# Down-projection of a hybrid decoder layer: the last group's right columns as seven products instead of eight

## The chip, the cores and the metric

The kernel runs on one core of a Trainium2 chip. The metric is device time in microseconds (us) of one execution. Before the change it is 1039.08 us, the median of three runs (1039.08 to 1039.49). The profiled execution took 1039.66 us, of which 1037.9 us lie between its first and its last instruction (the span).

## The reference

One decoder layer, all in float32, 256 positions, width 2048, hidden width 5632:

```python
h = rmsnorm(x, g_mix)
z = h @ w_in                       # gated conv, causal pooling, cross-attention
x = x + concat(conv, pool, att) @ w_out
h = rmsnorm(x, g_ffn)
u = causal_dwconv(h @ w_up, ffn_conv_w) + ffn_conv_b
gate, val = split(u, 2)
x = x + (silu(gate) * val) @ w_down
return rmsnorm(x, g_final)
```

The change touches only the last matrix product, `(silu(gate) * val) @ w_down`: 256 rows by 5632 by 2048.

## The kernel before, in words

**Numbers.** TensorE (PE) multiplies in a reduced float32 form. So every float32 operand is split into two, hi and lo = x - hi, and a product of two operands is three matmuls: hi by hi, hi by lo, lo by hi. One matmul takes a 128x128 stationary block (activations) and streams a 128x512 block (weights). For each weight tile of 128 x 2048 elements (4 x 512), ScalarE (ACT) writes hi and VectorE (DVE) then writes lo; this is "the split" of a tile.

**The stream.** All weight tiles stand in one list, `stream`, in the order in which PE uses them. `next_tile` takes the next one; before it does, it issues the loads up to three tiles ahead and the splits up to two ahead (`LOAD_AHEAD`, `SPLIT_AHEAD`). hi and lo have three buffers each, so the split of tile k can only begin when PE is through with tile k - 3. Tiles of `w_up` are loaded into the tag `raw`, three buffers too.

**Up-projection.** The hidden width is cut into 11 units of 512 (`UNITS` = 2, 2, 2, 2, 2, 1 units in six groups). One unit is eight tiles: four for the gate half (w = 0), then four for the value half (w = 1). One tile is 24 matmuls (`up`, line 981): two blocks of 128 rows, four inner blocks, three matmuls each. After the fourth tile of a half, ACT copies PSUM to z and `up_finish` is put on the list `todo`; it is taken off that list after the next tile's first row block. `up_finish` turns z on PE (eight transposes `pz`, line 1079), runs the three-tap convolution on ACT and DVE (lines 1087 and 1089), and multiplies gate and value.

**Down-projection of five groups.** A group of two units gives an activation block of 256 rows by 1024, and its part of `w_down` is 1024 by 2048. That is taken as two blocks of columns, p = 0 (left 1024) and p = 1 (right 1024). Within one, activations (a11, a12, a21, a22) and weights (b11, b12, b21, b22) are 2x2 blocks, and seven products replace eight. `make_forms` builds the sums of activations once per group, `sums`: index 0 is a11, 1 to 4 are sums, 5 is a12, 6 is a22, and for the last group 7 is a21. One product is 12 matmuls (`prod`, line 921), after which DVE adds the PSUM result to `xt` or subtracts it (line 927).

**The weight sums** are made in place, in three buffers of the tile `ffn` (`rawd`), by `Blocks.split`. In order of the products 0 to 6 the split reads:

| product | reads | what its split issues afterwards |
|---|---|---|
| 0 | b11 | DVE: b11 += b12 (line 247); then POOL's queue: an accumulating DMA b12 += b22 from memory (line 244) |
| 1 | b11 + b12 | DVE: b11 += b22 |
| 2 | b11 + b12 + b22 | |
| 3 | b12 + b22 | SP's queue: load b21 over b12 (line 241); POOL's queue: accumulating DMA b11 += b21 |
| 4 | b22 | SP: load the next block's first part |
| 5 | b21 | SP: load the next block's second part |
| 6 | b11 + b12 + b22 + b21 | SP: load the next block's third part |

The next block's parts are b11, b22, b12 in that order; each goes into the buffer that has just been split, so b12 of a block waits for the split of product 6 of the block before.

**The last block** (group 4, p = 1) is of the class `Plain` before the change: four tiles b11, b21, b12, b22 as they are, each split with no sums (lines 281 and 282) and used by `plain` for both row blocks: 24 matmuls a tile (line 1127), 96 in all, and after every second tile two additions to `xt` (line 1136).

**The order around the change.** The list `sched` mixes the tiles of the last unit (u = 10, eight tiles here called U0 to U7) with the products of group 4. `after[t]` says how many products come behind tile t. Before, `after = [0, 0, 0, 1, 1, 1, 2, 6]`. With P0 to P6 the products of the left block and N0 to N3 the four plain tiles, PE's list is: U0 U1 U2 U3 P0 U4 P1 U5 P2 U6 P3 P4 U7 P5 P6 N0 N1 N2 N3. The forms of group 4 are built while U1 and U2 run, since the `up_finish` that completes them is taken off `todo` in U0. The `up_finish` of the last value half is taken off inside N0; it writes `u_last`, which `down_last` needs.

**The end.** `down_last` does the last unit's down-projection in plain form (four tiles, lines 501 to 507 and 1164 to 1166), the final norm and the output.

Which instruction stands where in the queue of PE, ACT and DVE is decided when the program is built, by a planner that goes by program order among what its own estimates show as ready; each engine then runs its queue strictly in that order. Only the first stage and `down_last` are written in a fixed order.

Of the kernel before, what the change touches and what calls it, by code (L numbers as in the profile page):

```python
# [24 lines left out]
def kernel(  # L25
# [25 lines left out]
    def bank(name):  # L51
        return psum.tile([P, 512], F32, tag="bank", name=name)
# [101 lines left out]
    def next_tile():  # L154
        i = state["use"]
        state["use"] += 1
        advance(i + 1 + LOAD_AHEAD, i + 1 + SPLIT_AHEAD)
        return split.pop(i)
# [46 lines left out]
    group_of = []  # L205
# [109 lines left out]
    blocks = []  # L315
    for gi in range(len(group_of) - 1):
        for p in range(2):

            kind = Plain if gi == len(group_of) - 2 and p == 1 else Blocks
            blocks.append(kind(len(blocks), gi, p))  # L320
            if len(blocks) > 1:
                blocks[-2].next = blocks[-1]
# [33 lines left out]
    for gi, (a, n) in enumerate(group_of):  # L356
        n_t = 8 * n
        if not prods:
            after = [0] * n_t
        elif n == 2:  # L360
            after = [0, 0, 0] + [1] * 12 + [2]
        else:
            after = [0, 0, 0, 1, 1, 1, 2, 6]
        assert sum(after) == len(prods)
        for t in range(n_t):
            if gi == 0:
                if t == 0:
                    for o in UP_ORDER:
                        sched.append(("up", 0, o) if isinstance(o, int) else ("mixed", UpBlocks.U, o[1]))
                continue  # L370
            sched.append(("up", a + t // 8, t % 8))
            for _ in range(after[t]):
                sched.append(prods.pop(0))
        if gi < len(group_of) - 1:
            prods = []
            for b in blocks[2 * gi : 2 * gi + 2]:
                n = len(b.ORDER) if isinstance(b, Plain) else N_PROD
                prods += [("plain" if isinstance(b, Plain) else "prod", b, i) for i in range(n)]
# [170 lines left out]
    for k in range(KC):  # L549
        i, j = divmod(k, 4)  # L550
# [347 lines left out]
            tt(form(at, 1), src, form(at, 0).bitcast(F32), op=ALU.subtract)  # L898
        tt(four(1), t, four(0).bitcast(F32), op=ALU.subtract)

    chains = {}

    def prod(bl, i):
        hi, lo = next_tile()

        chain, first, tb, right, op = (
            ("a", True, 0, 0, ALU.add),
            ("b", True, 1, 1, ALU.add),
            ("a", False, 0, 1, ALU.subtract),
            ("a", False, 1, 1, ALU.subtract),  # L910
            ("b", False, 0, 1, ALU.add),
            ("c", True, 0, 0, ALU.add),
            ("a", False, 1, 0, ALU.add),
        )[i]
        if first:
            chains[chain] = bank(f"pp_{bl.gi}_{bl.p}_{chain}")
        ps = chains[chain]
        for j in range(4):
            ah, al = bl.stationary(i, j)
            for n, (a, b) in enumerate(((ah, hi), (ah, lo), (al, hi))):  # L920
                nc.tensor.matmul(  # L921
                    ps, a, b[:, j, :], start=first and j == 0 and n == 0,
                    stop=j == 3 and n == 2, skip_group_check=True,
                )
        c0 = bl.p * 1024 + right * 512
        o = xt[:, tb, c0 : c0 + 512]
        nc.vector.tensor_tensor(o, o, ps, op=op)
# [13 lines left out]
    for o in out_sched:  # L941
        if o[0] == "prod":
            prod(out_blocks, o[1])
            continue
        n2, k, first, last = o
        if first:
            ps = [[bank(f"po_{n2}_{tb}_{n}") for n in range(2)] for tb in range(TB)]
            at_tile = 0
        mm_b(ps, next_tile(), mixT, (k, k + 1), range(TB), first, last)
        at_tile += 1  # L950
        if n2 == 0 and at_tile <= 3:
            out_blocks.load(("b11", "b22", "b12")[at_tile - 1])
        if n2 == 1 and at_tile in (2, 3):
            transpose_in(xt, h2T, "g_ffn", range((at_tile - 2) * 4, (at_tile - 1) * 4), "x2")
        if last:
            add_in(ps, n2 * 2, range(TB), f"o{n2}", ssq4)
# [5 lines left out]
    rawd = [ffn[:, 1 + i, :].rearrange("p (j c) -> p j c", c=512) for i in range(3)]  # L962

    u_last = h2T[:, : 4 * UNITS[-1], :]
    up_ps, up_gates, todo, r_2 = {}, {}, [], []

    def up(u, b):

# [266 lines left out]
    for what, a, b in sched:  # L1235
        {"up": up, "mixed": up_mixed, "prod": prod, "plain": plain}[what](a, b)
# [32 lines left out]
```

## Time and profile before

| what | value |
|---|---|
| median of three runs | 1039.08 us |
| profiled execution | 1039.66 us, span 1037.9 us |
| PE busy | 1026.7 us, 99% of the span |
| DVE busy | 820.5 us, 79% |
| ACT busy | 601.8 us, 58% |
| POOL busy | 64.1 us, 6% |
| DMA moved | 224.97 MB, 217 GB/s on average |
| granted TensorE clock | 0.997 of full speed |

A row of a view of groups gives the source line, the engine, the operation, what it writes and reads, how often, the busy time and the mean of one. A row of a timeline gives start and duration in us, and in square brackets how long the engine had been idle before, and what ended that. PE is the matmuls, PEld its weight loads, SPq the queue of DMA issues. A matmul's own duration (390 ns) is longer than the distance between two, since they overlap; the distance is read from the chain of waits, where 12 of 512 columns take 2.72 us.

### The profile page before, as it was taken

To read this page: it belongs to the slowest core of one execution; us is meant where nothing else is said; L and a number is where in the kernel's file an instruction comes from. 1 tells how busy PE (TensorE), PEld (TensorE's weight loads), DVE (VectorE), ACT (ScalarE), POOL (GpSimd) and SP (SyncE) were. 2 spreads that over 40 slices of the span, in tenths; PEclk is the share of its full clock that TensorE was granted. 3 is DMA by queue.
4 is the path that set the end of the run, shared out by engine and by line. 5 is a ranking of instruction groups with operands and counts; after the bars stand their busy time and mean duration, and the time that the engine had idled before them with its cause. 6 is when DMAs were issued, how large, how long until landed. Compare 5 with 4: busy or idle time off the path is not lost.

```text
span 1037.9 us, 12624 instructions
## 1 busy us (share of the span) xinstructions
PE 1026.7 (99%) x4970; PEld 861.9 (83%) x4970; DVE 820.5 (79%) x866; ACT 601.8 (58%) x654; POOL 64.1 (6%) x97
## 2 busy tenths in 40 slices
PE   9999999999999999999999999999999999999996
PEld 7888888888888888888888888888888888888885
DVE  5677686777869688978779787797878978789776
ACT  5965454544556576655556556665566655665653
POOL 0023500000001000000000000000000000000000
PEclk9999999999999999999999999999999999999998
DMA  9765465557775687687966878668786697867832
GB/s 321 254 214 191 146 201 175 191 191 240 220 262 176 155 259 243 197 253 203 259 224 201 255 204 260 219 199 258 208 260 216 194 265 209 258 218 191 282 118 81
DMA packets 125157, 224.97 MB, mean 217 GB/s; under 512 B 3970, under 2 KB 36010, under 8 KB 124970
## 3 DMA queue, kind: packets, MB, share of 16 engines
q1 hardware_dynamic: 113450, 201.09, 57.2%
q0 software_dynamic: 11616, 23.07, 13.6%
q8 instruction: 39, 0.64, 0.2%
q14 instruction: 20, 0.16, 0.1%
q10 hardware_dynamic: 32, 0.01, 0.0%
HBM read 222.06 MB, written 2.10 MB: 216 GB/s over the span
## 4 chain that ended last, share of the span: by engine, by line
PE 98%; DMA 1%; DVE 0%; SPq 0%; DVEq 0%; issue 0%; ACT 0%
PE pu L981 42%; PE pp_a L921 9%; PE pp_b L921 5%; PE pp_c L921 2%; PE pa_cb L468 2%; PE pa_pv L468 2%; PE pa_cx L468 2%; PE pa_cc L468 2%; PE po L504 2%; PE pp L1127 2%; PE po L501 2%; PE po L507 2%; PE pz L1079 2%; PE pm_a L1024 2%; PE pa_q L468 1%; PE pk L558 1%
## 5 line engine op out<-in xcount | busy, mean ns | idle before, releaser
L981 PE MATMUL pu<-hi,h2T 128*128 128x512 f32 x1280 | 409.4, 391 | 0.0
L132 DVE TENSOR_TENSOR lo<-raw,hi 128x2048 fp32r<-128x2048 f32 (+3 forms) x148 | 314.7, 2128 | 70.9 <-ACT hi L131 69.9
L131 ACT ACTIVATE hi<-raw 128x2048 fp32r<-128x2048 f32 (+3 forms) x148 | 264.3, 1789 | 110.5 <-issue 34.7
L981 PEld LDWEIGHTS pu<-hi,h2T 128*128 128x128 f32 x1280 | 240.3, 188 | 49.4
L981 PE MATMUL pu<-lo,h2T 128*128 128x512 f32 x640 | 249.5, 390 | 0.0
L255 DVE TENSOR_TENSOR lo<-ffn,hi 128x2048 fp32r<-128x2048 f32 x70 | 160.3, 2290 | 72.0 <-ACT hi L254 72.0
L254 ACT ACTIVATE hi<-ffn 128x2048 fp32r<-128x2048 f32 x70 | 134.0, 1916 | 105.1 <-PE pu L981 75.0
L981 PEld LDWEIGHTS pu<-lo,h2T 128*128 128x128 f32 x640 | 120.2, 188 | 25.1 <-DVE lo L132 0.7
L921 PE MATMUL pp_a<-hi,sums 128*128 128x512 f32 x288 | 94.5, 389 | 0.0
L1089 DVE SCALAR_TENSOR_TENSOR t<-pz,cols,t 128x255 f32<-128x255 f32 (+1 forms) x176 | 79.6, 478 | 10.2 <-ACT t L1087 9.2
L1087 ACT ACTIVATE t<-pz,cols 128x256 f32<-128x256 f32 x88 | 46.9, 558 | 48.1 <-DVE t L1089 24.2
L921 PEld LDWEIGHTS pp_a<-hi,sums 128*128 128x128 f32 x288 | 54.1, 188 | 11.2
L244 POOL DMA_DIRECT2D ffn<-in_w_down_dram x18 | 23.1, 1284 | 575.8 <-DVE ffn L247 454.3
L921 PE MATMUL pp_a<-lo,sums 128*128 128x512 f32 x144 | 56.0, 389 | 0.0
L1005 ACT ACTIVATE z<-pu,r_x 128x512 f32<-128x512 f32 x40 | 27.4, 686 | 39.7 <-PE pu L981 39.6
L247 DVE TENSOR_TENSOR ffn<-ffn 128x2048 f32<-128x2048 f32 x20 | 45.7, 2287 | 3.4 <-DMA ffn<-in_w_up_dram 3.4
L921 PE MATMUL pp_b<-hi,sums 128*128 128x512 f32 x144 | 47.3, 389 | 0.0
L921 PEld LDWEIGHTS pp_a<-lo,sums 128*128 128x128 f32 x144 | 27.0, 188 | 5.6
L921 PEld LDWEIGHTS pp_b<-hi,sums 128*128 128x128 f32 x144 | 27.0, 188 | 5.6
L468 PE MATMUL pa_cb<-hT,hi 128*128 128x512 f32 x96 | 30.7, 400 | 0.0
L468 PE MATMUL pa_pv<-hT,hi 128*128 128x512 f32 x96 | 30.2, 396 | 0.0
L468 PE MATMUL pa_cc<-hT,hi 128*128 128x512 f32 x96 | 30.2, 395 | 0.0
(292 smaller groups left out, 1477.1 us busy)
## 6 DMA issues: line engine op xcount, KB each, us to landing
raw<-in_w_up_dram SPq DMA_DIRECT2D x84, 1024.0 KB, 7.5
ffn<-in_w_down_dram SPq DMA_DIRECT2D x40, 1024.0 KB, 6.1
raw<-in_w_in_dram SPq DMA_DIRECT2D x28, 1024.0 KB, 5.0
ffn<-in_w_down_dram POOLq DMA_DIRECT2D x18, 1024.0 KB, 10.3
raw<-in_w_out_dram SPq DMA_DIRECT2D x12, 1024.0 KB, 5.1
raw<-in_w_kv_dram SPq DMA_DIRECT2D x4, 1024.0 KB, 7.3
outp<-in_w_out_dram SPq DMA_DIRECT2D x4, 1024.0 KB, 7.5
ffn<-in_w_up_dram SPq DMA_DIRECT2D x4, 1024.0 KB, 5.5
```

The costliest lines, as they stand in the source:

```text
L131: nc.scalar.activation(hi[:, s, :], raw[:, s, :], AF.Copy)
L132: nc.vector.tensor_tensor(lo[:, s, :], raw[:, s, :], hi[:, s, :].bitcast(F32), op=ALU.subtract)
L244: nc.gpsimd.dma_start(self.buf(to), self.source(what), accum_op=ALU.add)
L247: nc.vector.tensor_tensor(self.buf(to), self.buf(to), self.buf(what), op=ALU.add)
L254: nc.scalar.activation(hi, raw, AF.Copy)
L255: nc.vector.tensor_tensor(lo, raw, hi.bitcast(F32), op=ALU.subtract)
L468: nc.tensor.matmul(ps[mi], hi[:, kk, c], actT[:, k, :], start=first and kk == 0, stop=False)
L921: nc.tensor.matmul(ps, a, b[:, j, :], start=first and j == 0 and n == 0, stop=j == 3 and n == 2, skip_group_check=True,)
L981: nc.tensor.matmul(ps[tb], x_, y_[:, kk, :], start=k == 0 and n == 0, stop=k == KC - 1 and n == 2,)
L1005: nc.scalar.activation(z[tb], ps[tb], AF.Copy, scale=r_2[0][:, tb : tb + 1])
L1087: nc.scalar.activation(t, v, AF.Identity, bias=cvec("ffn_conv_b", m), scale=cw[2])
L1089: nc.vector.scalar_tensor_tensor(t[:, s:], v[:, : S - s], cw[2 - s], t[:, s:], op0=ALU.mult, op1=ALU.add)
```

## The change

The class of the last block becomes `Blocks` like that of the nine before it, so its weights are summed and split by the table above and its seven products (here Q0 to Q6) go through `prod`. The list `after` of the last unit is spread anew for 14 products instead of 7 products and 4 plain tiles. PE's list becomes: U0 U1 U2 P0 U3 P1 U4 P2 P3 U5 P4 P5 U6 P6 Q0 U7 Q1 Q2 Q3 Q4 Q5 Q6, and then `down_last`. The pending `up_finish` is taken off `todo` in Q2, behind its matmuls. The class `Plain`, the function `plain` and the form of index 7 stay in the file; nothing uses the first two, and the form is still made.

```diff
@@ -315,8 +315,7 @@
     for gi in range(len(group_of) - 1):
         for p in range(2):
-
-            kind = Plain if gi == len(group_of) - 2 and p == 1 else Blocks
+            kind = Blocks
             blocks.append(kind(len(blocks), gi, p))
@@ -360,7 +359,7 @@
         elif n == 2:
             after = [0, 0, 0] + [1] * 12 + [2]
         else:
-            after = [0, 0, 0, 1, 1, 1, 2, 6]
+            after = [0, 0, 1, 1, 2, 2, 2, 6]
         assert sum(after) == len(prods)
@@ -898,7 +897,7 @@
-    chains = {}
+    chains, todo = {}, []
@@ -922,6 +921,8 @@
                     stop=j == 3 and n == 2, skip_group_check=True,
                 )
+        if todo and bl.gi == len(group_of) - 2 and bl.p == 1 and i == 2:
+            todo.pop(0)()
         c0 = bl.p * 1024 + right * 512
@@ -962,7 +963,7 @@
-    up_ps, up_gates, todo, r_2 = {}, {}, [], []
+    up_ps, up_gates, r_2 = {}, {}, []
```

## The prediction
> **What bounds the kernel now.** I read the page first, then the chain of waits around the change, then the stretch before and within the last unit by engine.
>
> ```profile
> span 1037.9 us, 12624 instructions
> PE 1026.7 (99%) x4970; PEld 861.9 (83%) x4970; DVE 820.5 (79%) x866; ACT 601.8 (58%) x654; POOL 64.1 (6%) x97
> ```
>
> ```profile
> 942.72 2.72 PE pp_a L921 x12
> 945.44 0.23 PE pu L981
> ...
> 951.81 2.72 PE pp_b L921 x12
> 954.53 5.44 PE pu L981 x24
> ...
> 981.73 2.72 PE pp_a L921 x12
> 984.45 2.72 PE pp L1127 x12
> 987.17 0.88 PE pz L1079 x8
> 988.05 19.05 PE pp L1127 x84
> 1007.11 0.45 PE pl L501 x2
> ```
>
> PE has no gap: each piece starts where the last one ended. So one product of 12 matmuls is 2.72 us, a tile of 24 is 5.44 us, and any wait put on PE lengthens the kernel by itself. P0 starts at 942.72, so U3, 24 matmuls, began at 937.28 and U2 ended there. U4 with its eight transposes runs from 945.44 to 951.81: 6.37 us. The last down-projection starts at 1007.11; what follows it is not touched, so the sum is made on this one point.
>
> ```profile
> 920.00:937.30 17.30, 17.30 (x82) 14.40 (x81) 17.06 (x26) 9.92 (x12) 0.00 (x0) 1.00 0.56 183
> 937.30:1007.10 69.80, 69.80 (x317) 57.89 (x317) 59.83 (x54) 40.97 (x37) 2.56 (x2) 1.00 0.66 196
> ```
>
> By stretches (length, then busy time of PE, PEld, DVE, ACT, POOL, then granted clock, DMA share and GB/s), DVE is not at its mean of 79% here. While U1 and U2 run it is busy 17.06 of 17.30 us, and in the last unit 59.83 of 69.80 us. Its work there, not its average, decides what can be added.
>
> **Removed.** Four plain tiles are 96 matmuls, seven products are 84. Twelve matmuls at 2.72 us per twelve: **-2.72 us** of PE. With nothing else, the down-projection would start at 1004.4. Splits, additions to `xt` and loads of the plain tiles go too, but are replaced.
>
> **Added.** The durations:
>
> ```profile
> L254 ACT ACTIVATE hi<-ffn x70: 1897/1917/1925, 333.3 to 974.3; 128x2048 fp32r<-128x2048 f32 x70
> L255 DVE TENSOR_TENSOR lo<-ffn,hi x70: 2282/2292/2294, 335.6 to 977.2; 128x2048 fp32r<-128x2048 f32 x70
> L247 DVE TENSOR_TENSOR ffn<-ffn x20: 2284/2286/2292, 341.2 to 948.6; 128x2048 f32<-128x2048 f32 x20
> L927 DVE TENSOR_TENSOR xt<-xt,pp_a 128x512 f32<-128x512 f32 x4 | 2.7, 681 | 0.0
> L241 SPq DMA_DIRECT2D ffn<-in_w_down_dram x40: 367/368/368, 377.3 to 983.9; - x40
> DMA to landing us min/median/max: 5.1/6.1/7.7
> L244 POOL DMA_DIRECT2D ffn<-in_w_down_dram x18: 1282/1282/1303, 425.2 to 956.4; - x18
> DMA to landing us min/median/max: 9.2/10.3/11.9
> ```
>
> Seven splits instead of four, two weight additions (line 247) and seven additions to `xt` instead of four. On DVE that is 3 x 2.29 + 2 x 2.29 + 3 x 0.68 = 13.5 us; in the second stretch DVE had 69.80 - 59.83 = 10.0 us idle. So DVE alone can eat the gain: with 2.7 us less room, 16.2 us would have to go into 10.0 us and what can be done after the down-projection has begun. ACT gets 3 x 1.92 = 5.8 us more and had 28.8 us idle there; that is hidden. Two accumulating DMAs (b22 and b21 a second time, 1 MB each) come to POOL's queue, which stood empty after 956.4 us; at 196 GB/s and a DMA share of 0.66 in that stretch there is room for 2 MB.
>
> **The wait at U3.** P0 and P1 come one tile earlier. This is what DVE and ACT did there:
>
> ```profile
> 928.89 2.29 DVE L132 TENSOR_TENSOR lo<-raw,hi 128x2048 fp32r<-128x2048 f32 x1
> ...
> 936.43 0.69 DVE L895 TENSOR_TENSOR turn<-turn,ffn 128x512 f32<-128x512 f32 x1
> 937.03 2.29 DVE L255 TENSOR_TENSOR lo<-ffn,hi 128x2048 fp32r<-128x2048 f32 x1
> 939.23 2.29 DVE L899 TENSOR_TENSOR sums<-turn,sums 128x2048 fp32r<-128x2048 f32 x1
> 941.43 2.29 DVE L247 TENSOR_TENSOR ffn<-ffn 128x2048 f32<-128x2048 f32 x1
> 943.63 2.29 DVE L132 TENSOR_TENSOR lo<-raw,hi 128x2048 fp32r<-128x2048 f32 x1
> 945.84 2.29 DVE L255 TENSOR_TENSOR lo<-ffn,hi 128x2048 fp32r<-128x2048 f32 x1
> ```
>
> ```profile
> 937.15 1.92 ACT L896 ACTIVATE sums<-turn 128x2048 fp32r<-128x2048 f32 x1 [2.26 <-DVE turn L895]
> 943.82 1.92 ACT L254 ACTIVATE hi<-ffn 128x2048 fp32r<-128x2048 f32 x1 [0.37 <-DVE ffn L247]
> ```
>
> In order: lo of U3, the forms up to line 895, lo of P0, the rest of the forms (line 899), the weight addition behind P0, lo of U4, lo of P1. After the change the tile split at 928.89 is P0, and U3's lo comes into the place of 937.03. PE then wants U3 at 940.0 (2.72 us after 937.28) and P1 at 945.4. P1 needs lines 899 and 247 and its own hi and lo. If DVE keeps the order of the rows (U3's lo, 899, 247), 247 ends at 943.7 as now, hi follows to 945.6, lo to 947.9: **P1 waits 2.4 us**. If 247 and 899 go ahead of U3's lo, that ends at 943.6 and U3 waits 3.6 us. If nothing stood between, P1's lo could end at 945.8: 0.4 us. I take 2.4, the order of the rows; the ends 0.4 and 3.6 stay for the range. From here all of PE is 2.4 us later.
>
> **The chain through the weight buffers.** This is the term that decides. In the plain block each tile lasts 5.44 us on PE and needs one load; now Q1 to Q6 stand together at 2.72 us each and hang on each other through memory. Followed from P6:
>
> P6's split waits for a free buffer, the end of P4. P4 would end at 968.1 without a wait (937.28, plus four products and U3, U5 at 2.72 and 5.44, U4 at 6.37, and P4), so at 970.5. hi and lo, 1.92 + 2.29: 974.8. Only then is b12 loaded, 6.1 us: 980.9. DVE adds it to b11, 2.29: 983.2. Then the accumulating DMA b12 += b22, issued 0.3 us later, as this row stands against the end of line 247 at 943.72, and 10.3 us long: 993.8.
>
> ```profile
> 944.02 1.28 POOL L244 DMA_DIRECT2D ffn<-in_w_down_dram  x1 [56.56 <-DVE ffn L247]
> ```
>
> Q3's split, 4.2 us: 998.0. Only then is b21 loaded over it, 6.1 us: 1004.1. Q5's split, 4.2 us: 1008.4. Q5 and Q6, 5.44 us: the down-projection starts at **1013.8**. PE on its own would reach Q5 at 1003.4 (U7 waits for its lo to 985.4, Q1 ends 993.5, Q2's lo ends at 994.0 after b11 += b22, Q3 begins at 998.0, Q4 ends 1003.4), and so stands still for about 5 us before Q5. The sum: -2.72 for the matmuls, +2.4 before P1, +2.2 in small waits from U7 to Q3, +5.0 before Q5, which is 6.9; by the chain 1013.8 - 1007.1 = **+6.7 us**, which I take.
>
> Cover that I count as nothing: the second accumulating DMA (b11 += b21) starts behind Q2's lo at 994.3 and lands at 1004.6, while Q6's hi can start at 1006; if Q5 were on time, this one would hold Q6. For the left block the same steps end in time: b11 += b22 behind P1's lo ends at 950.1, P2's split at 954.3 (when b12 += b22, issued at 944.0, has landed too), P3's at 958.5 against 959.7 on PE; b21 lands at 964.6, before P5's buffer is free. On SP's queue the late load of b21 stands in front of what is issued later, the last tile of the down-projection and the final gains; those need `raw` buffers freed by later splits anyway. On POOL's queue nothing stands behind. On DVE, b11 += b12 waits for b12's landing with the lo of U7 behind it (or ahead of it: then the chain is 2.1 us later, an end for the range; I take the addition first, as in program order). The last `up_finish` starts behind Q2:
>
> ```profile
> 999.74 0.42 DVE L602 TENSOR_TENSOR h2T<-t,h2T 128x256 fp32r<-128x256 f32 x1
> ```
>
> Before, from the transposes at 987.17 to this row, its last, 13.0 us; behind Q2 at 996.6 it ends at 1009.6, four us ahead of the down-projection. Without the wait at Q5 it would be next in line: 992.6 + 13.0 = 1005.6 against 1004.4, so 1.2 us of the 2.7 would go there.
>
> **Ends of the unknown costs.** The two loads 5.1 to 7.7 each, the accumulating DMA 9.2 to 11.9, the early wait 0.4 to 3.6, the order on DVE 0 to 2.1. All at the low end: 6.7 - 1.0 - 1.0 - 1.1 - 2.0 = +1.6 us. All at the high end: 6.7 + 1.6 + 1.6 + 1.6 + 1.2 + 2.1 = +14.8 us. Neither is likely as a whole; about half of either side leaves +3.5 to +10.5.
>
> **Rivals.** A change of under 0.2% (2.1 us) counts as no change, about what a measurement of this kernel can tell.
>
> *The gate on the clock adds to it.* These are stretches after PE's last matmul:
>
> ```profile
> 1028.91 0.28 PE L1166 MATMUL pl<-hi,h2T 128*128 128x256 f32 x1
> ...
> 1031.00:1032.00 1.00, 0.00 (x0) 0.00 (x0) 0.93 (x4) 0.00 (x0) 0.00 (x0) 0.77 0.68 262
> 1032.00:1033.00 1.00, 0.00 (x0) 0.00 (x0) 1.00 (x2) 0.00 (x0) 0.00 (x0) 0.50 0.20 72
> ```
>
> About 2.3 us after PE stopped, its granted clock fell from 1.00 to 0.50. A wait of 5 us before Q5 is longer than that, so Q5 and Q6 could run at half speed: between 0 and 5.44 us more, since no row shows how soon the clock returns. I take the middle, 2.7: +9.4, **1048.5 us**. Against it: if the wait is split into two shorter ones, nothing falls. The Trainium skill, "TensorE: Matmul & The Clock Gate", section "Part 1: The HAM clock gate", says the clock halves after an idle window of about 3.4 us and comes back after as long a busy one. The fall after 2.3 us here is within such a free-running window; by the rule Q5 would lose up to 1.7 us (an estimate from that page), which makes 1047.5.
>
> *All of it is hidden, faster.* Then only the matmuls count: -2.72, or -1.5 with the wait for `up_finish`: 1036.4 to **1037.6 us**. For it: PE has no wait in the whole last unit now, though there ACT did wait for a plain tile's load:
>
> ```profile
> 982.96 1.92 ACT L281 ACTIVATE hi<-ffn 128x2048 fp32r<-128x2048 f32 x1 [1.42 <-DMA ffn<-in_w_down_dram]
> ```
>
>  It decides only if the chain from P6's lo to Q5, 33.6 us, is covered; by the walk PE wants Q5 28.6 us after it (974.8 to 1003.4), and 26.6 us after it with no wait on the way (972.3 to 998.9). It would take both loads and the accumulating DMA at their shortest, the early wait gone, and more.
>
> *Same.* All terms at the low end, +1.6: **1040.7 us**.
>
> *The block doesn't run as seven products in this order.* The planner could move a down-projection tile ahead of Q5; its hi and lo need the buffer of Q4, so little is won, and the last stage has its order written out. I give this nothing of its own.
>
> **How the numbers follow.** The profiled execution took 1039.66 us, 1.76 more than its span, and the median is 0.58 below it. +6.7 gives a span of 1044.6, a profiled execution of 1046.4 and a median of **1045.8 us**. Chances: this chain without the clock 0.52 (its own range 1042.5 to 1049.5), with the clock 0.30 (to 1051.5), worse than that 0.04, same 0.07, faster 0.07. So slower by over 0.2%: 0.86. The range that leaves out less than 2 in 10 runs from the low end of the chain to the chain with the clock: 1040.6 to 1051.5 us.
>
> **What would show it.** In the changed kernel: matmuls of the last block 84, PE busy lower by about 2.7 us while the span is longer; in the chain of waits a step from the accumulating DMA to Q3's hi and one from the load of b21 to Q5's hi, with PE idle 4 to 6 us before Q5; a wait of DVE or ACT for lo or line 247 of 1 to 4 us around 940 to 948; `up_finish` off the chain; perhaps a clock below 1.00 after the wait. It is wrong if PE stays without gaps from U3 to the down-projection, if b12 or b21 of the last block lands before PE wants it, or if the longest wait is for DVE's backlog and not for memory.

## The result, and the profile after

The changed kernel takes **1057.85 us** (median of four runs, 1056.15 to 1058.28) against 1039.09 us for the kernel before on the same chip: a ratio of 1.0176, with a 95% interval of 1.0163 to 1.0188. It is slower by 18.8 us. The forecast was 1045.8 us with a range up to 1051.5: the direction was right, the size was not.

The profiled execution took 1058.03 us, its span is 18.4 us longer than before. The first rows of the profile's page, and its shares of the chain that ended last:

```profile
span 1056.3 us, 12617 instructions
PE 1032.5 (98%) x4958; PEld 864.0 (82%) x4958; DVE 832.8 (79%) x874; ACT 606.7 (57%) x657; POOL 66.7 (6%) x99
PE 87%; DVE 5%; DMA 4%; ACT 2%; issue 1%; SPq 0%; DVEq 0%; ACTq 0%; POOLq 0%
```

The twelve matmuls are gone (4970 to 4958), yet PE is busy for 5.8 us *more*: some matmuls ran at a lower clock. The DMA share of the chain, 4%, lies almost entirely in the last 80 us. This is the chain of waits of the changed kernel there (start, length, what):

```profile
943.48 6.88 PE pu L982 x22
...
975.59 2.21 DVE lo L255
977.80 0.02 issue
977.82 6.22 DMA ffn<-in_w_down_dram
...
986.73 11.42 DMA ffn<-in_w_down_dram
...
1000.17 2.30 DVE lo L255
1002.48 0.02 issue
1002.49 10.41 DMA ffn<-in_w_down_dram
...
1014.95 2.29 DVE lo L255
```

Read from top to bottom: U3's matmuls; P6's lo; the load of b12, landed at 984.04; the accumulating DMA b12 += b22, behind an addition on DVE, landed at 998.15; Q3's lo; the load of b21, landed at 1012.90; Q5's lo. The skeleton is the one that the prediction walked. The last down-projection began at 1007.11 us before. Now its first two matmuls slip in among the first of Q6, but the first that reads a lo part stands at 1025.43 us, behind Q6; before, that one stood at 1007.56, so it is 17.9 us later, nearly the whole difference. PE's own gaps, from its timeline of the changed kernel:

```profile
940.62 0.73 PE L982 MATMUL pu<-hi,h2T 128*128 128x512 f32 x2 [0.92 <-ACT hi L131]
942.42 0.50 PE L920 MATMUL pp_b<-hi,sums 128*128 128x512 f32 x1 [1.07 <-ACT hi L254]
943.48 0.53 PE L982 MATMUL pu<-lo,h2T 128*128 128x512 f32 x1 [0.56 <-DVE lo L132]
...
988.51 0.50 PE L920 MATMUL pp_b<-hi,sums 128*128 128x512 f32 x1 [1.03 <-ACT hi L254]
999.52 0.50 PE L920 MATMUL pp_a<-lo,sums 128*128 128x512 f32 x1 [1.74 <-DVE lo L255]
1004.72 0.50 PE L920 MATMUL pp_b<-lo,sums 128*128 128x512 f32 x1 [2.15 <-DVE lo L255]
...
1014.97 0.50 PE L920 MATMUL pp_c<-hi,sums 128*128 128x512 f32 x1 [3.16 <-ACT hi L254]
1017.29 0.80 PE L920 MATMUL pp_c<-lo,sums 128*128 128x512 f32 x1 [1.82 <-DVE lo L255]
```

Two groups: 2.6 us before U3, and some 10 us from Q1 on. Those gaps are 12.5 us; with the 2.7 us of matmuls saved there are some 8 us more to find. Most of them are matmuls that ran slower, as the stretches show (length, busy time of PE, PEld, DVE, ACT, POOL, granted clock, DMA share, GB/s):

```profile
944.00:948.00 4.00, 4.00 (x13) 3.13 (x12) 4.00 (x3) 0.29 (x2) 0.00 (x0) 0.60 1.09 238
...
1000.00:1016.00 16.00, 10.16 (x36) 7.30 (x34) 10.07 (x14) 6.72 (x11) 1.19 (x1) 0.88 0.59 133
1016.00:1020.00 4.00, 2.71 (x6) 2.15 (x7) 4.00 (x8) 3.88 (x3) 0.00 (x0) 0.50 0.00 0
1020.00:1024.00 4.00, 4.00 (x14) 3.20 (x13) 4.00 (x4) 1.56 (x1) 0.00 (x0) 0.71 0.00 0
```

The granted clock is 0.60 behind the wait at U3 and 0.50 to 0.71 while Q5 runs. Both had to be tested, since a low clock beside a wait may or may not cost anything.

### The profile page after: what moved, and what is told of

Its sections match the earlier page's. It is cut to its first block, busy times and chain, and to the rows that moved or that the text cites. A ratio compares the mean times of both kernels' runs of the same rounds, so it can differ in the third digit from the quotient of the medians.

```text
span 1056.3 us, 12617 instructions
## 1 busy us (share of the span) xinstructions
PE 1032.5 (98%) x4958; PEld 864.0 (82%) x4958; DVE 832.8 (79%) x874; ACT 606.7 (57%) x657; POOL 66.7 (6%) x99
## 4 chain that ended last, share of the span: by engine, by line
PE 87%; DVE 5%; DMA 4%; ACT 2%; issue 1%; SPq 0%; DVEq 0%; ACTq 0%; POOLq 0%
PE pu L982 38%; PE pp_a L920 8%; PE pp_b L920 4%; DMA ffn<-in_w_down_dram 3%; PE pa_cb L467 2%; PE pa_cc L467 2%; PE pa_pv L467 2%; PE pa_cx L467 2%; PE po L506 2%; PE po L500 2%; PE po L503 2%; PE pp_c L920 2%; PE pz L1080 2%; PE pm_a L1025 2%; PE pa_q L467 1%
## 5 line engine op out<-in xcount | busy, mean ns | idle before, releaser
L255 DVE TENSOR_TENSOR lo<-ffn,hi 128x2048 fp32r<-128x2048 f32 x77 | 176.1, 2289 | 78.4 <-ACT hi L254 78.4
L254 ACT ACTIVATE hi<-ffn 128x2048 fp32r<-128x2048 f32 x77 | 147.4, 1915 | 109.2 <-PE pu L982 69.0
L920 PE MATMUL pp_a<-hi,sums 128*128 128x512 f32 x320 | 105.8, 392 | 0.0
L920 PEld LDWEIGHTS pp_a<-hi,sums 128*128 128x128 f32 x320 | 60.7, 190 | 13.1 <-DVE xt L928 0.2
L920 PE MATMUL pp_a<-lo,sums 128*128 128x512 f32 x160 | 62.8, 393 | 1.7 <-DVE lo L255 1.7
L247 DVE TENSOR_TENSOR ffn<-ffn 128x2048 f32<-128x2048 f32 x22 | 50.3, 2285 | 7.3 <-DMA ffn<-in_w_up_dram 3.7
L920 PE MATMUL pp_b<-hi,sums 128*128 128x512 f32 x160 | 53.4, 394 | 2.1 <-ACT hi L254 2.1
L920 PEld LDWEIGHTS pp_a<-lo,sums 128*128 128x128 f32 x160 | 30.3, 189 | 8.2 <-DVE lo L255 2.0
L920 PE MATMUL pp_b<-lo,sums 128*128 128x512 f32 x80 | 31.5, 394 | 2.1 <-DVE lo L255 2.1
L920 PE MATMUL pp_c<-hi,sums 128*128 128x512 f32 x80 | 27.9, 411 | 3.2 <-ACT hi L254 3.2
## 6 DMA issues: line engine op xcount, KB each, us to landing
ffn<-in_w_down_dram POOLq DMA_DIRECT2D x20, 1024.0 KB, 10.4
```

The lines of the kernel that those rows point to most:

```text
L247: nc.vector.tensor_tensor(self.buf(to), self.buf(to), self.buf(what), op=ALU.add)
L254: nc.scalar.activation(hi, raw, AF.Copy)
L255: nc.vector.tensor_tensor(lo, raw, hi.bitcast(F32), op=ALU.subtract)
L920: nc.tensor.matmul(ps, a, b[:, j, :], start=first and j == 0 and n == 0, stop=j == 3 and n == 2, skip_group_check=True,)
```

## The experiments

Four suspects came out of this comparison: the early wait at U3, the chain through memory, the clock, and DVE's queue at the end. The experiments take them apart one by one. Line numbers move by a few where an edit adds lines.

### The early wait alone

The kernel before, with its four plain tiles, and only the list changed: P0 to P3 come one tile earlier, so that P0 and P1 stand where the change has them.

```diff
-            after = [0, 0, 0, 1, 1, 1, 2, 6]
+            after = [0, 0, 1, 1, 1, 1, 1, 6]
```

> The kernel before with its four plain tiles, and only the list of places changed: products start one tile earlier (0, 0, 1, 1, 1, 1, 1, 6), the end of the list as before. Theory (VectorE's backlog in front of U3, about 3.7 us of waiting, and a lower granted clock for the tile after it, about 1.9 us; TensorE has no slack later that could swallow it): 1044 to 1045.5 us. Rival (the early wait is made up later, and only the chain through memory costs): within 1 us of 1039.1.

Measured: 1044.01 us (1043.93 to 1044.18), ratio 1.0044 (1.0027 to 1.0060): **+4.9 us** from the order of the list alone (4.7 against the runs of the kernel before that were taken beside it), twice the 2.4 us of the prediction. In the timeline of DVE of the changed kernel one sees why:

```profile
936.73 2.29 DVE L247 TENSOR_TENSOR ffn<-ffn 128x2048 f32<-128x2048 f32 x1
938.93 2.29 DVE L898 TENSOR_TENSOR sums<-turn,sums 128x2048 fp32r<-128x2048 f32 x1
941.14 2.29 DVE L132 TENSOR_TENSOR lo<-raw,hi 128x2048 fp32r<-128x2048 f32 x1
```

The weight addition and the rest of the forms both went *ahead of* U3's lo. That is the bad end (3.6 us) of the prediction; it took the other order because the rows of before had it. The planner did not keep that order once the tiles were moved.

The opposite edit, the changed kernel with its list begun later:

```diff
-            after = [0, 0, 1, 1, 2, 2, 2, 6]
+            after = [0, 0, 0, 1, 2, 2, 3, 6]
```

> The changed kernel with the list (0, 0, 0, 1, 2, 2, 3, 6): P0 comes behind U3 as in the kernel before, Q0 to Q6 stand where the change put them. Theory (early wait and chain through memory add up, since the chain starts from P6): about 5.5 us less than the change, 1051 to 1054 us. Rival (the chain is tied to something that does not move with TensorE's early wait, such as the accumulating DMAs): 1056 to 1058 us.

Measured: 1054.62 us (1054.37 to 1054.93), ratio 1.0146 (1.0130 to 1.0161): 3.2 us less than the change, not 4.9. The early gaps shrink to two of 0.56 and 0.48 us further on. Yet the chain through memory begins only 1.7 us sooner (P6's lo ends at 976.07 us, not at 977.80), and the accumulating DMA b12 += b22 happened to take 9.02 us in this profile, not 11.42; so not even the whole 3.2 us can be put down to the list. Of the 18.8 us at most 4.9 are this wait.

### The clock

e1 has the early wait and nothing else, so the clock can be tested there: sixteen matmuls whose result nobody reads stand in the gap before U3 and keep PE running.

```diff
+        if u == n_units - 1 and b == 3:
+            fill = bank("fill")
+            for _ in range(16):
+                nc.tensor.matmul(
+                    fill, h2T[:, 0, :P], h2T[:, 1, :], start=True, stop=True
+                )
```

> The kernel of the first experiment (four plain tiles, products one tile earlier), with 16 matmuls of 512 columns that nobody reads put between P0 and U3, 16 x 0.227 = 3.6 us, into a bank of their own; the wait before U3's second matmul was about that long. The output is unchanged. Theory (the tile behind the wait ran at a lower granted clock because TensorE had stood nearly still; 22 matmuls of U3 took 6.5 instead of 5.0 us): with the wait filled the clock stays at 1.00, U3 takes 5.0 us, and the time falls by 1.2 to 1.8 us to about 1042.5 us. Rival (U3 is slow for another reason, its operands for instance, and the record of the clock only goes with it): the same 1044.0 us or up to 0.5 us more.

Measured: 1042.97 us (1042.76 to 1044.47), ratio 1.0038 (1.0026 to 1.0051): 1.0 us less than e1. The runs of the two overlap, so the saving rests on the chains of waits as well. First that of e1, then that of the kernel with the fill:

```profile
943.59 6.47 PE pu L981 x22
```

```profile
940.00 3.63 PE fill L978 x16
...
944.31 4.99 PE pu L987 x22
```

The same 22 matmuls take 6.47 us behind a gap and 4.99 us behind the fill, where the granted clock is 1.00 in every stretch; the fill itself made U3 begin 0.7 us later. So of the 4.9 us, one to one and a half are the clock, the rest is the wait for DVE. The Trainium skill, "TensorE: Matmul & The Clock Gate", section "Part 1: The HAM clock gate", lists the halved clock as the state after an idle window of about 3.4 us. Here it fell although PE's single gaps were 0.9, 1.1 and 0.6 us with one or two matmuls between them, so a sparse stretch can be enough, and the window, read as one gap, would have missed it.

It does not fall every time. Ten of the profiles have these three gaps, the last of them 0.26 to 0.56 us long (the change, e1, e3, e4, e11 and e13 to e17). In eight the clock fell to about 0.50 behind them, and 22 matmuls took 6.47 to 7.84 us where the chain of waits shows them together. In e14 and e16 it stayed at 1.00 with the same gaps, and they took 5.30 us. The code is the same in this stretch, so one execution can differ from the next by one and a half us or more here, and small differences of medians below have to be read with that in mind.

The same idea in the tail of the changed kernel, 36 unread matmuls in the waits before Q2, Q4 and Q5:

```diff
+            if bl.seq == 9 and i == 5 and j == 0:
+                for _ in range(36):
+                    nc.tensor.matmul(
+                        ps, sums[:, 0, 0, 0, :], h2T[:, 5, :], start=True, stop=True,
...
+                    )
```

> The changed kernel with 36 matmuls that nobody reads, written into Q5's bank before its first product; by the program 9 of them stand in the wait before Q2's second matmul, 7 before Q4's and 20 before Q5. The output is unchanged. Theory (the clock that fell in the waits of the last products costs about 2 us at Q4 and Q3 and about 2 us at Q5, but Q6 waits for its lo until 1021.8 us anyway): the granted clock stays near 1.00 there and the time falls by 1 to 3 us. Rival (the waits end when memory and VectorE deliver, whatever the clock): within 0.7 us of the change, or slower by the matmuls put in.

Measured: 1057.84 us (1055.35 to 1058.75), ratio 1.0172 (1.0156 to 1.0188). The clock rose to 1.00 throughout the tail, and **the time did not move**. The stretches of this kernel, beside those of the changed one above:

```profile
1016.00:1020.00 4.00, 3.05 (x12) 2.17 (x12) 4.00 (x8) 3.70 (x4) 0.00 (x0) 1.00 0.00 0
1020.00:1024.00 4.00, 2.76 (x12) 2.31 (x13) 4.00 (x4) 1.47 (x1) 0.00 (x0) 1.00 0.00 0
```

From 1020 to 1024 PE is busy for 2.76 us where it had been busy for 4.00: it runs faster and then waits. What it waits for is the subject of the last group of runs.

### The chain through memory

First, one accumulating DMA out: b11 += b21 is not read from memory a second time but added on DVE, after Q5's split, from the b21 that has been loaded for Q5.

```diff
-                self.add_far("b11", "b21")
+                if self.seq != 9:
+                    self.add_far("b11", "b21")
+            elif idx == 5 and self.seq == 9:
+                self.add("b11", "b21")
```

> The changed kernel, but in the last block the second accumulating DMA (b11 += b21 from memory) is left out and VectorE adds b21 from its buffer, behind Q5's split. Theory (the load of b21 took 10.4 us instead of 6 because it ran beside that accumulating DMA): the load lands in 5.5 to 6.5 us, and the time falls by 3 to 4 us, to about 1054 us. Rival (a load at this place takes about 10 us by itself): the load still takes 9 to 10.5 us, and the time stays or rises by up to 2.5 us for the addition.

Measured: 1058.59 us (1056.21 to 1059.97), ratio 1.0181 (1.0166 to 1.0196): no gain. That is the rival's time, but not for the rival's reason, since the load did get shorter. Its rows hold the largest single finding. The chain of waits, DVE and PE of this kernel:

```profile
1003.76 6.11 DMA ffn<-in_w_down_dram
```

```profile
1015.91 2.29 DVE L247 TENSOR_TENSOR ffn<-ffn 128x2048 f32<-128x2048 f32 x1
```

```profile
1020.28 0.51 PE L923 MATMUL pp_a<-hi,sums 128*128 128x512 f32 x1 [3.21 <-ACT hi L254]
```

The same load of b21 takes **6.11 us alone and 10.41 us beside the accumulating DMA** that the change issues at 999.91. The 4.3 us won there are lost again, because the addition on DVE stands behind what `up_finish` has in the queue, starts only at 1015.91, and Q6 waits 3.21 us for it. Behind that wait the granted clock is 0.55 to 0.59, and eleven matmuls of Q6 take 4.56 us instead of 2.5. No run puts a plain load in the place of the accumulating DMA, so whether any second transfer would cost as much stays open.

That price stood in the trace of before as well. Here are its DMA issues between 944 and 954 us (KB each, median us to landing), the stretch in which the accumulating DMA of 944.02 runs:

```profile
ffn<-in_w_down_dram POOLq DMA_DIRECT2D x1, 1024.0 KB, 10.5
raw<-in_w_up_dram SPq DMA_DIRECT2D x1, 1024.0 KB, 9.9
raw<-in_w_down_dram SPq DMA_DIRECT2D x1, 1024.0 KB, 5.2
```

A plain load of the same 1024 KB, issued 1.9 us after the accumulating DMA: 9.9 us; one issued 1.4 us before that DMA ended: 5.2. The prediction had used the median of all loads of line 241, 6.1 us.

Next, both plain loads off the chain: b12 of the last block goes early into a buffer that is free by then (`u_raw`), b21 into the buffer that P6 frees; both accumulating DMAs stay.

```diff
             if idx == 0:
                 self.add("b11", "b12")
                 self.add_far("b12", "b22")
+                if last:
+                    self.next.load("b12")
...
-                names = Plain.ORDER if isinstance(self.next, Plain) else ("b11", "b22", "b12")
+                names = ("b11", "b22", "b21" if last else "b12")
                 self.next.load(names[idx - 4])
...
+    class Last(Blocks):
+
+        def buf(self, name):
+            if name == "b12":
+                return u_raw.rearrange("p c t -> p (c t)").rearrange("p (j c) -> p j c", c=512)
+            return rawd[self.at(name)]
...
+            elif idx == 3:
+                self.add_far("b11", "b21")
```

In `Last`, the class of the last block, nothing loads b21 behind Q3's split any more.

> The changed kernel, but the last block's b12 has a buffer of its own (the activations' buffer, free once the forms are built) and is loaded while the left block runs; b21 goes into the buffer that P6 frees, right behind P6's split. Both accumulating DMAs stay. Theory (the chain of loads through one buffer is what holds Q3 and Q5): the load of b12 (6.2 us) and that of b21 (10.4 us) leave the chain; what is left is one accumulating DMA in front of Q3; 1043 to 1046 us with the early wait still in it. Rival (VectorE's backlog or the accumulating DMAs set the end): above 1050 us.

> The experiment with a buffer of its own for b12, and the list (0, 0, 0, 1, 2, 2, 3, 6), so P0 again behind U3. Theory (early wait and what is left of the chain add up): the 4.5 to 5.5 us of the early wait go, 1050.3 to about 1045 to 1046 us. Rival (the second accumulating DMA and VectorE's queue hold the end wherever the block begins): 1048 to 1051 us.

Measured: 1050.26 us (1049.47 to 1052.43), ratio 1.0107 (1.0092 to 1.0122), with the list as changed; 1049.52 us (1048.44 to 1050.07), ratio 1.0097 (1.0083 to 1.0111), with the later list. So the two serial loads are worth **7.6 us**, but the theory had expected 1043 to 1046: something else stands at 1050. And the late list, which had won 3.2 us, now wins no more than 0.7: the costs do not add up, and there is a second floor below the memory.

The bound for all of memory: no accumulating DMA and no load of b21 in the last block; DVE adds b22 in both places and the split of Q3 and Q5 reads b22.

```diff
+            last = self.seq == 9
+            names = ("b11", "b11", "b11", "b12", "b22", "b21", "b11")
+            if last:
+                names = ("b11", "b11", "b11", "b22", "b22", "b22", "b11")
...
+            if last:
+                if idx < 2:
+                    self.add("b11", "b22")
```

> The changed kernel, but the last block does without memory in its sums: both accumulating DMAs and the load of b21 are left out, VectorE's two additions stay but add b22, which lies there in time, and Q3 and Q5 read b22 (so the right half of the output is not the reference's). Splits, additions to xt, products and list are those of the change. Theory (of the 18.8 us, 4.7 are the early wait and the rest is the chain through memory, less 2.7 for the matmuls): the chain goes, 1041 to 1045 us. Rival (dense splits, three buffers of hi and lo and VectorE's queue hold the last six products anyway): 1048 us or more.

> The same without memory in the last block's sums (output of the right half not the reference's), with the list (0, 0, 0, 1, 2, 2, 3, 6). Theory: both costs of the change are gone, what is left is the 2.7 us of matmuls against small waits: 1037 to 1040 us. Rival (as before): 1043 us or more.

Measured: 1049.02 us (1048.56 to 1049.14), ratio 1.0089 (1.0072 to 1.0106), and with the later list 1049.27 us (1047.53 to 1052.51), ratio 1.0097 (1.0074 to 1.0119). The rival held in both. **All of memory is worth 8.8 us** (1057.85 less 1049.02), 7.6 of them in the two plain loads. What stays in e11 is 10 us above the kernel before, with no transfer in the chain of waits from U3 to the down-projection (b12 is still loaded, but nobody reads it). With the later list (e12) that chain still goes through two loads, b21 of the left block (8.56 us) and b22 of the last one (6.14), so the bound is e11.

An attempt to keep the sums right and yet off the DMA queues: b12 early as in e4, and both accumulations as additions on POOL from what is already on the chip, with two lists.

```diff
+        def add_pool(self, to, what):
+            nc.gpsimd.tensor_tensor(self.buf(to), self.buf(to), self.buf(what), op=ALU.add)
...
-                self.add_far("b12", "b22")
+                self.add_pool("b12", "b22")
...
-            elif idx == 3:
-                self.add_far("b11", "b21")
+            elif idx == 2:
+                self.add_pool("b11", "b21")
```

The lines are set against e4 with the later list. The form of index 7, which nothing reads, is not built either.

> As the kernel with b12 in its own buffer and the later start, but in the last block both accumulating DMAs are left out: b12 += b22 and b11 += b21 are added on POOL from the buffers, and the form of index 7, which nobody reads, is not built. Theory (what is left is the accumulating DMAs, 10 to 11 us each from issue, against about 4 to 6 us for the addition on POOL by eight times the 0.6 us that 128x256 took there): 1038 to 1042 us. Rival (VectorE's own work, 13.5 us more in a stretch with 10 us idle, is the bound): 1043 us or more.

> As the kernel with the sums on POOL, with the list (0, 0, 0, 1, 1, 3, 4, 5): five products instead of six behind U7, three between U5 and U6, four between U6 and U7. Theory (with memory off the chain the order matters little as long as each split has time): within 1.5 us of the kernel with the sums on POOL. Rival (the dense products in front of U7 wait for b21 and for VectorE as Q1 to Q6 did): 2 to 5 us slower than it.

Measured: 1057.21 us (1056.53 to 1058.29), ratio 1.0176 (1.0160 to 1.0192), and 1058.36 us (1055.93 to 1059.25), ratio 1.0180 (1.0166 to 1.0194). As slow as the change. POOL and DVE of the first of them:

```profile
981.63 6.59 POOL L250 TENSOR_TENSOR ffn<-ffn 128x2048 f32<-128x2048 f32 x1 [25.57 <-DVE ffn L247]
```

```profile
981.46 2.29 DVE L132 TENSOR_TENSOR lo<-raw,hi 128x2048 fp32r<-128x2048 f32 x1
...
984.25 6.11 DVE L258 TENSOR_TENSOR lo<-ffn,hi 128x2048 fp32r<-128x2048 f32 x1
```

POOL's addition lasts 6.59 us, and beside it a lo that takes DVE 2.29 us takes 6.11. The rows show the two taking turns: POOL's began 0.17 us after a lo on DVE, which ended at 983.75; from there to POOL's end at 988.22 it is 4.47 us, and DVE's next lo, begun at 984.25, ends 2.14 us behind that. In e10, where no such row ran on DVE when POOL began, the addition takes 4.54 us, within the 4 to 6 that had been expected. So the engines do not work side by side here: the two additions of e8 hold DVE up by 3.8 us and by 4.4 us (three lo in 11.06 us from 995.20 on), and what leaves memory comes back as time of DVE. The Trainium skill, "SBUF — State Buffer", section "Who interferes with whom", says that a DVE instruction with two inputs from SBUF contends with a GpSimd (POOL) instruction that reads SBUF; these rows agree.

### What stays without memory

In e11 the last product comes late, though its data are on the chip. DVE of that kernel, then PE:

```profile
1002.09 2.28 DVE L259 TENSOR_TENSOR lo<-ffn,hi 128x2048 fp32r<-128x2048 f32 x1
1004.29 1.64 DVE L1097 SCALAR_TENSOR_TENSOR t<-pz,cols,t 128x255 f32<-128x255 f32 x4
...
1010.23 2.29 DVE L259 TENSOR_TENSOR lo<-ffn,hi 128x2048 fp32r<-128x2048 f32 x1
```

```profile
1010.25 0.73 PE L507 MATMUL pl<-hi,h2T 128*128 128x512 f32 x2 [1.39 <-ACT hi L131]
1012.57 0.61 PE L927 MATMUL pp_a<-lo,sums 128*128 128x512 f32 x1 [1.36 <-DVE lo L259]
```

From the end of Q5's lo (1002.09 and 2.28 us on) to the start of Q6's (1010.23) 5.9 us pass on DVE, nearly all with rows of the last `up_finish` and one pause of 0.57 us inside it. PE waits 1.39 and 1.36 us in two gaps before Q6's lo and then runs Q6 at a granted clock of 0.60. The test: the eight taps (line 1097 there) of the last value half are left out.

```diff
-            for s in (1, 2):
+            for s in (1, 2) if (u, w) != (10, 1) else ():
```

> The kernel without the last block's memory chain (label e11_no_memory_chain, 1049.02 us), with the eight tap instructions of the last value half left out on DVE as well, so the last half's convolution has one tap of three and the output is not the reference's. There DVE's rows run without a gap from 1004.29 to 1010.23 through six taps, four multiplications and three lo parts of up_finish, and the last product's lo comes only then (1010.23 to 1012.52), though its hi had been ready since 1007.02. Theory: the 8 us that stay without memory come mostly from DVE's queue, in which the last up_finish stands between the splits. Eight taps of about 0.40 us each are 3.2 us; the last product then starts 3 us sooner, and without the slower clock behind the wait perhaps 4: 1045 to 1046 us. Rival: the buffers of hi and lo and the planner's order set the end (the last product's hi waits for the matmuls of Q3, 1.87 us), so DVE is only where the wait shows: 1048 us or more.

Measured: 1045.00 us (1043.93 to 1046.31), ratio 1.0057 (1.0042 to 1.0072): **4.0 us** less than e11, for eight instructions of 0.4 to 0.5 us. From Q2's first matmul to the first of the down-projection that reads a lo part the profiles have 21.8 us in e11 and 17.5 in e14, so the gain lies in this stretch. The two lo now follow each other without a row between, and the clock stays at 1.00:

```profile
1002.70 4.49 DVE L259 TENSOR_TENSOR lo<-ffn,hi 128x2048 fp32r<-128x2048 f32 x2
```

Leaving out work also let the planner change the order of the last rows, so the 4.0 us are the price of the taps in this place, order included. The next run leaves nothing more out than e11 and only moves the step: `up_finish` comes off its list behind Q1, not Q2.

```diff
-        if todo and bl.gi == len(group_of) - 2 and bl.p == 1 and i == 2:
+        if todo and bl.gi == len(group_of) - 2 and bl.p == 1 and i == 1:
```

> The kernel of e11_no_memory_chain (output's right half not the reference's, as there), in which the last up_finish is taken off its list one product sooner: behind Q1's matmuls, not Q2's. Nothing is left out beside that; the taps move up in DVE's queue by about one split. Theory (up_finish and the dense splits share one queue): part of the queue's work moves into the idle 2 us of DVE before 993.50, so 1 to 3 us are won: 1046 to 1048 us. Rival (the splits are bound by buffers): 1049, within 1 us.

Measured: 1048.97 us (1048.60 to 1049.55), ratio 1.0095 (1.0080 to 1.0110), against 1049.02: nothing. PE's long wait has only moved from Q6 to Q5:

```profile
1009.79 0.50 PE L927 MATMUL pp_c<-lo,sums 128*128 128x512 f32 x1 [2.32 <-DVE lo L259]
```

So my theory held in its core (the work in DVE's queue sets the end) but not in its corollary: the work did not move into DVE's idle stretch. The 2.04 us in front of 994.25 are idle in this run too, and the taps still stand among the splits, from 999.26 us on. Whether another place would fill that stretch was not tried.

Finally, back to the changed kernel with all its memory: the taps left out, and then the taps left out *and* the 36 unread matmuls of e13.

> The changed kernel with its whole memory chain, the eight taps of the last value half left out (the last half's convolution has one tap of three, the output is not the reference's). There the last product's lo ran at 1019.54, behind Q5's lo (1014.95) and what up_finish had left for DVE. Theory: memory sets Q5 (lo until 1017.24), but the 2.3 us until the last product's lo are DVE's queue; without the taps the last product comes 2 us sooner: 1055 to 1056.5 us. Rival: the last product waits for its own memory (the second accumulating DMA) or a buffer, and the taps are covered by the waits: 1057.5 us or more.

> The changed kernel with both of the last two edits that gained nothing by themselves: the eight taps of the last value half left out (as in e16_no_taps, 1056.73 us; the output is not the reference's) and the 36 unread matmuls in the waits of the tail (as in e13_fill_tail, 1057.84 us, clock 1.00 throughout). From the end of Q5's lo to the first matmul of the down-projection that reads the lo part the traces show 8.2 us in the changed kernel (1017.24 to 1025.43), 8.1 in e16 with half the clock in Q5, 7.8 in e13 with DVE's queue ahead of Q6. Theory: the slower clock and DVE's queue cover each other there, either is enough to hold Q6; without both that stretch is two products, 5.5 us, and the time comes to 1054 to 1055.5 us. Rival: a third thing holds Q6 (its memory, its hi's buffer), the stretch stays above 7 us and the time at 1056.5 or more.

Measured: 1056.73 us (1055.58 to 1058.01), ratio 1.0174 (1.0157 to 1.0191), a median 1.1 us lower with runs that overlap those of the change, so no gain that can be told from none; and 1055.35 us (1053.47 to 1056.98), ratio 1.0158 (1.0144 to 1.0172). The medians of e13 (four executions) and e17 (five) differ by 2.5 us, with runs that overlap. The stretch that the two edits act on shows it without that spread: from the end of Q5's lo to the first matmul of the down-projection that reads a lo part. Two products, 5.4 us, and two matmuls of the down-projection, 0.45 us, have to fit into it. The chain of waits in e16 shows Q5's matmuls at half the clock, with Q6's lo ready in time:

```profile
1015.34 4.91 PE pp_c L920 x11
```

and PE in e17 shows the first of Q5's lo matmuls and the first of the down-projection:

```profile
1016.54 0.50 PE L926 MATMUL pp_c<-lo,sums 128*128 128x512 f32 x1 [1.82 <-DVE lo L255]
...
1021.98 0.62 PE L500 MATMUL pl<-hi,h2T 128*128 128x512 f32 x2
```

In e17 the two products take 1021.98 less 1016.54, 5.44 us, without a wait. The whole stretch is 8.2 us in the change (1017.24 to 1025.43), 8.2 in e16 (1015.29 to 1023.46), 7.8 in e13 (1016.60 to 1024.38) and 6.0 in e17 (1016.49 to 1022.44). **Each of the two hides the other**: at half clock Q5 lasts as long as DVE needs to get to Q6's lo, and where the clock is restored PE waits for that lo. Taken away one at a time, each seems to cost nothing.

No kernel here is faster than the one before: the best version of the change that computes all of the layer is e4 with the later list, 10 us slower.

## Why the prediction was wrong in size

The prediction's chain against the chain of the profile, in us from the span's start; the last column is what that step adds to the miss of 11.6 us at the start of the down-projection:

| step | predicted | measured | adds |
|---|---|---|---|
| matmuls removed | 12 | 12 | 0 |
| P6's lo ends, b12's load starts | 974.8 | 977.8 | 3.0 |
| b12 landed | 980.9 (6.1) | 984.0 (6.2) | 0.1 |
| b12 += b22 landed | 993.8 (10.3) | 998.1 (11.4) | 1.2 |
| Q3's lo ends | 998.0 | 1002.5 | 0.1 |
| b21 landed | 1004.1 (6.1) | 1012.9 (10.4) | 4.3 |
| Q5's lo ends | 1008.4 | 1017.2 | 0 |
| down-projection starts | 1013.8 (5.4) | 1025.4 (8.2) | 2.8 |

**Where it was right.** The direction: a slower kernel, since in the last block the weight sums hang on each other through memory; which loads and accumulations stand on that chain and in which order; the addition of b12 ahead of U7's lo on DVE (984.14 and 986.35); the left block's chain in time for PE, though its b21, also loaded beside an accumulating DMA, took 9.3 us and landed at 967.3 us instead of 964.6. The signs it named came: fewer matmuls in a longer span, the accumulating DMA ahead of Q3's hi and the load of b21 ahead of Q5's in the chain, a wait before Q5 (3.16 and 1.82 us, together 5.0), a clock below 1.00. That the wait has the length of the forecast is luck: PE came to Q5 at 1011.8 us instead of 1003.4, and b21 landed 8.8 us late. One sign did not come: `up_finish` was to be off the chain, and its rows stand in it, from 1017.24 us on. That two loads, 7.6 us, are the greater part of the memory's cost is shown by e4.

**First failed step, the load of b21: "Only then is b21 loaded over it, 6.1 us".** It took 10.4 us. The duration was the median of a group over the whole kernel, and its bounds were that group's extremes, 5.1 and 7.7. But the next paragraph had the second accumulating DMA start at 994.3 and land at 1004.6, that is, across this very load, and counted it as cover that costs nothing. e3 shows 6.11 us with that neighbour gone. The row that prices the pair was in the trace of before, under another line number: a load of a different tensor with the same 1024 KB, 9.9 us beside an accumulating DMA. This is the largest term, 4.3 us, and it also makes the range too short, since both its ends came from loads in quieter company. That a stretch has room at 196 GB/s and a share of 0.66 said nothing about two transfers that meet.

**Second, "P1 waits 2.4 us".** e1 shows 4.9 us. I took the order of DVE's rows as they stood, though the edit moves a tile in the planner's list and the planner orders anew; the 3.6 us of the other order were in the text as the upper end. The rest, one to one and a half us, is the clock behind the gaps (e9), which the prediction had only considered before Q5. That is most of the first 3.0 in the table: PE was through with P4 at 973.27 us, where the walk had 970.5, so P6's split began 2.8 us late. An `xt` addition ahead of P6's lo on DVE (974.91), which the walk had left out, costs about 0.1, since P6's hi ends only at 975.44.

**Third, "Q5 and Q6, 5.44 us" and `up_finish` "four us ahead of the down-projection".** The end of `up_finish` was the wrong thing to look at. It had been counted as work with a due time of its own, whereas its rows stand *in* the queue in which Q6's lo stands. In the trace of the change Q6's lo runs at 1019.54, behind five rows of `up_finish`; in e11, with memory out, it is the last thing that PE waits for, and e14 shows that eight taps are worth 4.0 us there. This is also why the removal of all memory leaves 10 us: by the matmuls and the early wait of e1 alone e11 would have come to 1041.3 us (1039.1 - 2.7 + 4.9). The prediction had noted that DVE has 10.0 us idle for 16.2 us of work, and then let the walk along the memory chain decide alone. e11 and e14 show that this line would have been a bound in its own right, 8.8 us behind the memory.

**The rival with the clock** was named, with 2.7 us and a chance of 0.30. The size nearly came out: Q5 did run at half the clock, and the last stretch grew by 2.8 us, of which 0.45 are the two matmuls of the down-projection that now lie inside it. Its place on the path did not: with the clock restored (e13) the time is the same, because DVE's queue holds Q6 as long. It counts only together with the taps (e17). So the time lies above even this rival's range for the other reasons.

**What adds up.** From the change downwards: two plain loads off the chain, -7.6 us (e4); the rest of memory, -1.2 (e11); eight taps out of DVE's queue, -4.0 (e14, with the clock that this restores). That leaves 1045.0 us against 1036.4 by the matmuls alone (1039.1 - 2.7): 8.6 us, of which 4.9 are the early wait by e1. The last 3.7 us were not tried singly and stay open; in e14's trace PE has one more gap of 0.27 us at U5 and two of 1.33 and 0.28 us in the tail. The steps are not independent: the late list wins 3.2 us with memory in and 0.7 or nothing with less of it (e2, e7, e12).

## What to carry to other kernels

Price a transfer by a transfer in the same company: look for the stretch of the trace in which the same two kinds of DMA overlap, whatever their line, and do not take a group's median or even its extremes when the edit makes them meet. When a chain has been found that sets the end, walk the busiest engine's queue over the same stretch as well, row by row, for what stands in front of the last operand; taking the first bound away then costs an experiment less. And test a low clock, or any suspect beside another, both alone and together with it: two waits of equal length hide each other, and each alone looks free.

## What the runs showed of the hardware

- A load of 1 MB takes 6.1 us alone (e3) and 10.4 us beside an accumulating DMA of 1 MB (the change); in the kernel before 9.9 beside one and 5.2 when issued 1.4 us before its end. The accumulating one took 8.9 to 11.9 us in the kernel before and in the changed one.
- A float32 addition of 128x2048, both inputs on the chip, takes POOL 4.54 us (e10) and DVE 2.29 us, but not at the same time: in e8 POOL's took 6.59 behind a lo that DVE had begun, and DVE's next lo 6.11 behind POOL's. Moving such additions to POOL gained nothing.
- The granted clock can fall without one long gap: gaps of 0.9, 1.1 and 0.6 us with one or two matmuls between them brought it to about 0.50 in eight of ten profiles, and 22 matmuls then took 6.5 to 7.8 us; in the other two it stayed at 1.00 and they took 5.3. Matmuls that nobody reads, put in the gap, held it at 1.00 (e9, e13).
